# FFN-down of a decoder trunk: sums of the seven-product squares formed by GpSimd transfers in a two-slot ring, a fourth pair of half buffers, and 8, 8, 8, 5 squares for 7, 7, 7, 4

## The chip, the cores and the metric

The kernel runs on one core of one Trainium2 chip. The metric is the device time of one execution in microseconds; a measurement is the median of three runs. The core has a matrix engine (TensorE, "PE" in the profile, with its weight loads as "PEld"), three engines for elementwise work (VectorE "DVE", ScalarE "ACT", GpSimd "POOL"), a SyncE ("SP") that here issues nearly all DMA transfers, and 16 DMA engines that move data between HBM and the on-chip SBUF. TensorE accumulates into PSUM banks. Each engine works through its own instructions in program order and waits on semaphores for what others make; a stall of one instruction holds everything queued behind it on that engine.

## The reference

One decoder layer over 256 tokens of width 2048, in float32. The change lies in the channel mixer:

```python
h2 = rms_norm(x, mlp_norm[i])
x = x + jnp.square(jax.nn.relu(h2 @ w_ffn_up[i])) @ w_ffn_down[i]
```

with `w_ffn_up` 2048x8192 and `w_ffn_down` 8192x2048. Ahead of it come two mixers (causal pooling and an RWKV-7 recurrence) and the product with `w_out`; behind it

```python
gate = jax.nn.sigmoid(rms_norm(x, ple_norm[i]) @ w_ple_gate[i])
x = x + gate * (p[i] @ w_ple_proj[i])
return rms_norm(x, final_norm)
```

## The kernel before, in words

**Products.** All large products run as split float32: a weight block is divided into a high half (ScalarE copy, rounded to fp32r) and a low half (VectorE: raw minus high), and each product is three 128x512 matmuls (high·high, high·low, low·high). A weight block thus costs one load, ScalarE time for its high half, VectorE time for its low half, and TensorE time.

**Order.** The Python code records the instructions; a scheduler lays them out per engine by priority, so that the splits of later blocks (raised priority, `tc.high_priority(20000)`) move ahead of other work. What one engine then does is a fixed list. Loads of weights go through `load_raw` on SP into a small rotating set of buffers.

**FFN.** `ffn_half(hf)` runs twice, for 4096 hidden columns each. It first makes eight `y` tiles (`gemm_wide`, up-projection, squared ReLU, split), and then two `down_sweep(hf, pair)`; `pair` is one half of the output columns (0 to 1023, or 1024 to 2047). In tile names, `d01` is half 0, pair 1, and a number behind it is the step, `kp`. A sweep has 16 steps. Step `kp` takes a 256x1024 piece of `w_ffn_down` as four quarter blocks of 128x512 (here w11, w12 from the upper 128 rows, w21, w22 from the lower) against two row blocks of activations for each of two token tiles (a11, a12; a21, a22). Done plainly these are eight products, 24 matmuls.

**Squares.** In some steps, those in `SEVEN`, the piece is multiplied in the Strassen-Winograd way: seven products of sums of blocks, 21 matmuls. The four sums of activations are made once for a half by `activation_sums` and used in both sweeps. The sums of weights (t1, t2, t3, t4 in the code) are made at each square by four VectorE instructions on 128x512 (lines 1269 to 1272) in the tile `td`; a square has seven quarter blocks to split where a plain step has four. Before the change 7, 7, 7 and 4 steps of the four sweeps are squares, 25 of 64. In the last sweep, `d11`, only steps 1, 3, 7 and 11 are.

**Buffers.** Split halves of a step sit in rotating pairs of tiles (`wh`, `wl` in pool `wp`, three pairs), one tile pair called "a", "b", "c", "d" after the place in a step. The last pair of a square, "d", is held instead in two tiles with the tag `graw`. Those two tiles also take loads that `keep` makes during `d11`, at its 6th, 9th, 12th and 15th step: the last quarter of `w_ple_gate`, loaded early (line 1170), split into `gk` tiles (lines 1174, 1175) that take over `y` tiles no longer needed.

**End of a sweep.** After its last square the four banks that hold only products of squares are folded into the residual `x` (the `add` calls); in `d11` the first half of the transposes for the gate follow there.

## Time and profile before

| | |
|---|---|
| median of 3 runs | 1180.36 us (1180.09 to 1181.29) |
| time of the profiled execution | 1180.25 us |
| its span, first to last instruction | 1178.2 us |
| mean granted TensorE clock | 0.998 |
| TensorE busy | 1162.5 us, 99% |
| VectorE busy | 873.3 us, 74% |
| ScalarE busy | 709.3 us, 60% |
| GpSimd busy | 13.7 us, 1% |

Engine times are sums over one profiled execution. A "busy" TensorE is one with some matmul in flight, so the share says that it never lacked work for long, and the number and the pitch of the matmuls set the time. By the timeline, the four down sweeps run from 557.9 us to about 728 us (`d00`, `d01`) and from about 903 us to about 1076 us (`d10`, `d11`), with the second up-projection between them and the gate behind. The first of the two up-projections starts after the product with `w_out`, which stands at about 330 us.

### The profile page before, as it was taken

To read this page: it belongs to the slowest core of one execution; us is meant where nothing else is said; L and a number is where in the kernel's file an instruction comes from. 1 tells how busy PE (TensorE), PEld (TensorE's weight loads), DVE (VectorE), ACT (ScalarE), POOL (GpSimd) and SP (SyncE) were. 2 spreads that over 40 slices of the span, in tenths; PEclk is the share of its full clock that TensorE was granted. 3 is DMA by queue.
4 is the path that set the end of the run, shared out by engine and by line. 5 is a ranking of instruction groups with operands and counts; after the bars stand their busy time and mean duration, and the time that the engine had idled before them with its cause. 6 is when DMAs were issued, how large, how long until landed. Compare 5 with 4: busy or idle time off the path is not lost.

```text
span 1178.2 us, 17287 instructions
## 1 busy us (share of the span) xinstructions
PE 1162.5 (99%) x6419; PEld 973.4 (83%) x6419; DVE 873.3 (74%) x1188; ACT 709.3 (60%) x1309; POOL 13.7 (1%) x73
## 2 busy tenths in 40 slices
...
GB/s 290 154 202 146 135 140 119 119 179 157 160 203 178 177 182 196 184 192 200 187 204 212 198 202 209 186 191 191 185 195 190 202 205 195 290 233 249 197 56 72
DMA packets 60756, 216.81 MB, mean 184 GB/s; under 512 B 6784, under 2 KB 7552, under 8 KB 60288
## 3 DMA queue, kind: packets, MB, share of 16 engines
...
q14 instruction: 34, 0.28, 0.1%
...
## 4 chain that ended last, share of the span: by engine, by line
PE 96%; ACT 1%; DVE 1%; DMA 0%; issue 0%; SPq 0%; POOL 0%; DVEq 0%; POOLq 0%
PE u_w L1112 20%; PE u_w L1117 10%; PE d_b L1231 7%; PE d_b L1229 7%; PE d_b L1230 7%; PE d_w L1231 2%; PE d_w L1229 2%; PE d_w L1230 2%; PE gt_b L242 2%; PE gt_b L241 2%; PE gt_b L238 2%; PE zk_b L241 1%; PE zk_b L242 1%; PE o_b L241 1%; PE o_b L242 1%; PE zv_b L238 1%
## 5 line engine op out<-in xcount | busy, mean ns | idle before, releaser
L1112 PE MATMUL u_w<-h,wh_u 128*128 128x512 f32 x1024 | 321.9, 395 | 0.0
L167 ACT ACTIVATE wh_u<-raw_u 128x512 fp32r<-128x512 f32 x256 | 147.5, 623 | 160.9 <-issue 98.2
L168 DVE TENSOR_TENSOR wl_u<-raw_u,wh_u 128x1024 fp32r<-128x1024 f32 x128 | 156.6, 1224 | 105.2 <-ACT wh_u L167 103.5
L1117 PEld LDWEIGHTS u_w<-h,wl_u 128*128 128x128 f32 x1024 | 192.4, 188 | 45.4
L1117 PE MATMUL u_w<-h,wl_u 128*128 128x256 f32 x1024 | 201.4, 278 | 0.0
L1112 PEld LDWEIGHTS u_w<-h,wh_u 128*128 128x128 f32 x1024 | 156.0, 189 | 0.1
L168 DVE TENSOR_TENSOR wl_gt<-raw_gt,wh_gt 128x1024 fp32r<-128x1024 f32 x24 | 29.4, 1224 | 23.2 <-ACT wh_gt L167 23.2
L167 ACT ACTIVATE wh_gt<-raw_gt 128x512 fp32r<-128x512 f32 x48 | 28.0, 638 | 23.1 <-PE gt_b L242 14.4
L241 PE MATMUL gt_b<-wh_gt,h 128*128 128x512 f32 x96 | 37.3, 389 | 0.0
L242 PE MATMUL gt_b<-wh_gt,h 128*128 128x512 f32 x96 | 37.3, 389 | 0.0
L168 DVE TENSOR_TENSOR wl_o<-raw_o,wh_o 128x1024 fp32r<-128x1024 f32 x16 | 19.6, 1222 | 12.9 <-ACT wh_o L167 9.9
L167 ACT ACTIVATE wh_o<-raw_o 128x512 fp32r<-128x512 f32 x32 | 18.4, 623 | 16.3 <-issue 8.5
L167 ACT ACTIVATE wh_zp<-raw_zp 128x512 fp32r<-128x512 f32 x32 | 18.6, 623 | 15.7 <-PE zp_b L242 7.2
L168 DVE TENSOR_TENSOR wl_zk<-raw_zk,wh_zk 128x1024 fp32r<-128x1024 f32 x16 | 19.4, 1220 | 10.4 <-ACT wh_zk L167 10.4
L241 PE MATMUL zk_b<-wh_zk,hTh 128*128 128x512 f32 x64 | 25.2, 394 | 1.4 <-ACT wh_zk L167 1.4
L241 PE MATMUL zv_b<-wh_zv,hTh 128*128 128x512 f32 x64 | 26.0, 406 | 0.0
L167 ACT ACTIVATE wh_zk<-raw_zk 128x512 fp32r<-128x512 f32 x32 | 18.4, 622 | 12.4 <-PE zv_b L242 4.0
L241 PE MATMUL zp_b<-wh_zp,hTh 128*128 128x512 f32 x64 | 25.7, 401 | 0.0
L238 PE MATMUL gt_b<-wl_gt,h 128*128 128x512 f32 x96 | 25.7, 389 | 0.0
L168 DVE TENSOR_TENSOR wl_zv<-raw_zv,wh_zv 128x1024 fp32r<-128x1024 f32 x16 | 19.4, 1218 | 8.2 <-ACT wh_zv L167 7.4
L241 PE MATMUL zr_b<-wh_zr,hTh 128*128 128x512 f32 x64 | 25.4, 397 | 0.0
L242 PE MATMUL zp_b<-wh_zp,hTl 128*128 128x512 f32 x64 | 25.0, 391 | 0.0
...
## 6 DMA issues: line engine op xcount, KB each, us to landing
raw_u<-in_w_ffn_up_dram SPq DMA_DIRECT2D x128, 512.0 KB, 3.5
raw_d<-in_w_ffn_down_dram SPq DMA_DIRECT2D x128, 512.0 KB, 4.3
raw_gt<-in_w_ple_gate_dram SPq DMA_DIRECT2D x24, 512.0 KB, 3.5
raw_zk<-in_w_in_dram SPq DMA_DIRECT2D x16, 512.0 KB, 3.7
raw_zr<-in_w_in_dram SPq DMA_DIRECT2D x16, 512.0 KB, 3.3
raw_zv<-in_w_in_dram SPq DMA_DIRECT2D x16, 512.0 KB, 3.3
raw_zp<-in_w_in_dram SPq DMA_DIRECT2D x16, 512.0 KB, 3.2
raw_o<-in_w_out_dram SPq DMA_DIRECT2D x16, 512.0 KB, 4.2
```

The source lines that it names most:

```text
L167: nc.scalar.activation(wh[:, a * 512 : (a + 1) * 512], raw[:, a * 512 : (a + 1) * 512], AF.Copy)
L168: nc.vector.tensor_tensor(wl, raw, wh.bitcast(F32), op=ALU.subtract)
L238: nc.tensor.matmul(banks[tt], ah[:, ts_], halves[a][1], start=False, stop=last)
L241: nc.tensor.matmul(banks[tt], ah[:, ts_], halves[a][0], start=i + a == 0, stop=False)
L242: nc.tensor.matmul(banks[tt], al[:, ts_], halves[a][0], start=False, stop=False)
L1112: nc.tensor.matmul(bank[:, ct, :].rearrange("p (s t) -> p s t", s=2), wh[:, cs[ct]], hl, start=k == 0, stop=False, skip_group_check=True,)
L1117: nc.tensor.matmul(bank[:, ct, 0:T], wl[:, cs[ct]], hl[:, 0, :], start=False, stop=k == 15, skip_group_check=True)
L1229: nc.tensor.matmul(banks[n], ah, wh, start=first, stop=False)
L1230: nc.tensor.matmul(banks[n], ah, wl, start=False, stop=False)
L1231: nc.tensor.matmul(banks[n], al, wh, start=False, stop=last)
```

## The change

Numbers of lines are those of the new file where the new code is meant.

- **Which steps are squares.** `SEVEN` becomes (1, 3, 4, 6, 8, 9, 11, 13) for three sweeps and (1, 3, 6, 9, 11) for `d11`: 29 squares. Steps 3 and 4, and 8 and 9, are now neighbours in three sweeps. The order in which `d01` visits its steps is changed to (0, 2, 1, 5, 3, 4, 7, 6, 10, 8, 9, 12, 11, 14, 13, 15).
- **Sums of weights.** The seven products are rewritten so that one sum, p1 = w11 + w12, is the plain sum of two stored quarter blocks, and the others follow from it by two VectorE instructions: t2 = p1 − w22 on 128x512 (line 1309), in place in p1's memory, and t43, which subtracts t2 from both quarter blocks of rx (w21 and w11) at once, on 128x1024 with t2 read twice (line 1311), in place in rx. Signs move into the activation sum s3 and into a new constant `ns2` = −s2 for the two final adds.
- **How p1 is made.** GpSimd issues two transfers from HBM: one plain into a slot of `ring` (line 1228), and one that adds into the same slot (line 1229, `accum_op=ALU.add`), after waiting for the first. `ring` has two slots of 128x512; `begin_sum` starts two sums ahead of the FFN, and one more behind each square, for the square two further on. A square's second panel, `ry`, is loaded by SP with 256 KB for 512 KB.
- **Buffers.** Every fourth half pair lies in a pair of tiles of its own (`wh4`, `wl4`): four pairs for three. The memory of the tile `td` becomes the fourth tile for activation sums. The tile for w2 takes the place of the one for w11 and shares its memory with the activation sums' work tile (`junk`). The small tiles `ph`, `pl` become one, `phl`, in the ring's memory behind the FFN.
- **Order of products.** In a square 1, 2, 3, 5, 6, 4, 7 for 1, 2, 3, 5, 7, 6, 4. In a plain step the products with w21 come first, and the lower row panel is loaded first. `w_ffn_down` is laid out anew in HBM for that.

```diff
@@ -1157,6 +1157,7 @@
         nc.vector.reciprocal(s2, s2)
+        nc.vector.tensor_scalar_mul(ns2, s2, -1.0)
     h3_box = []
@@ -1185,28 +1186,56 @@
-    SEVEN = (1, 3, 5, 7, 9, 11, 13)
-    s_slots = (0, 2, 5)
+    SEVEN = (1, 3, 4, 6, 8, 9, 11, 13)
+    s_slots = (0, 2, 5, 1)
+    ns2 = const.tile([128, 2], F32, name="ns2")
     def activation_sums(box, kp, r):
         i = SEVEN.index(kp)
         if i % 2 == 0:
-            st = a8(s_slots[i // 2], f"S{kp}", F32R) if i < 6 else fp.tile([128, 1024], F32R, tag="S", name=f"S{kp}")
-            box[kp] = box[SEVEN[min(i + 1, len(SEVEN) - 1)]] = st
+            box[kp] = box[SEVEN[min(i + 1, len(SEVEN) - 1)]] = a8(s_slots[i // 2], f"S{kp}", F32R)
         st = box[kp][:, i % 2 * 1024 : i % 2 * 1024 + 1024]
...
-        nc.vector.tensor_tensor(s3, a11, a21, op=ALU.subtract)
+        nc.vector.tensor_tensor(s3, a21, a11, op=ALU.subtract)
         nc.vector.tensor_tensor(s2_, s1, a11, op=ALU.subtract)
-    def down_sweep(hf, pair, ys, sboxes, hooks=(), between=None, seven=SEVEN):
+    ring = fp.tile([128, 1024], F32, tag="S", name="ring")
+    squares_of = {}
+    visits_of = {}
+    for hf in range(2):
+        for pair in range(2):
+            last = hf + pair == 2
+            squares_of[hf, pair] = (1, 3, 6, 9, 11) if last else SEVEN
+            visits_of[hf, pair] = (0, 2, 1, 4, 3, *range(5, 16)) if last else (range(16), (0, 2, 1, 5, 3, 4, 7, 6, 10, 8, 9, 12, 11, 14, 13, 15))[pair]
+    in_line = [(*hp, kp) for hp, visits in visits_of.items() for kp in visits if kp in squares_of[hp]]
+    begun = []
+    turns = []
+    def slot(n):
+        return ring[:, n % 2 * 512 : n % 2 * 512 + 512]
+    def begin_sum():
+        n = len(begun)
+        if n < len(in_line):
+            hf, pair, kp = in_line[n]
+            nc.gpsimd.dma_start(slot(n), w_down[pair, hf * 16 + kp, 1, :, 1, :])
+            nc.gpsimd.dma_start(slot(n), w_down[pair, hf * 16 + kp, 0, :, 1, :], accum_op=ALU.add)
+            begun.append(n)
+    def summed(*square):
+        return slot(in_line.index(square))
+    def down_sweep(hf, pair, ys, sboxes, hooks=(), between=None):
         nm = f"d{hf}{pair}"
+        seven, visits = squares_of[hf, pair], visits_of[hf, pair]
         hooks = dict(hooks)
         b2, b4, b3, bx = (mm_bank(f"{nm}_b{i}") for i in range(4))
         w16, w57 = (wide_bank(f"{nm}_w{i}") for i in range(2))
@@ -1230,11 +1259,16 @@
             nc.tensor.matmul(banks[n], ah, wl, start=False, stop=False)
             nc.tensor.matmul(banks[n], al, wh, start=False, stop=last)
+        def half_tiles(name):
+            turns.append(name)
+            if len(turns) % 4 == 0:
+                return [fp.tile([128, 1024], F32R, tag=f"{hl}4", name=f"{hl}_{name}") for hl in ("wh", "wl")]
+            return [wp.tile([128, 1024], F32R, tag=hl, name=f"{hl}_{name}") for hl in ("wh", "wl")]
         def halves_of(src, name, own=False):
-            pool, kw = (fp, dict(bufs=2)) if own else (wp, {})
-            wh = pool.tile([128, 1024], F32R, tag="graw" if own else "wh", name=f"wh_{name}", **kw)
-            wl = pool.tile([128, 1024], F32R, tag="graw" if own else "wl", name=f"wl_{name}", **kw)
+            wh, wl = [fp.tile([128, 1024], F32R, tag="graw", bufs=2, name=f"{hl}_{name}") for hl in ("wh", "wl")] if own else half_tiles(name)
             with tc.high_priority(20000):
                 for c in range(2):
                     nc.scalar.activation(wh[:, c * 512 : c * 512 + 512], src[:, c * 512 : c * 512 + 512], AF.Copy)
@@ -1245,43 +1279,49 @@
             o = pair * 1024 + c * 512
             return xr[tt][:, o : o + 512]
-        def add(tt, c, src):
-            nc.vector.scalar_tensor_tensor(xs(tt, c), src, s2[:, tt : tt + 1], xs(tt, c), op0=ALU.mult, op1=ALU.add)
-        for q, kp in enumerate(((0, 2, 1, 4, 3, *range(5, 16)) if hf else (0, 2, 1, 4, 3, 6, 5, 8, 7, 10, 9, 12, 11, 14, 13, 15)) if pair else range(16)):
+        def add(tt, c, src, scale=s2):
+            nc.vector.scalar_tensor_tensor(xs(tt, c), src, scale[:, tt : tt + 1], xs(tt, c), op0=ALU.mult, op1=ALU.add)
+        def panel(kp, c, name, rows):
+            return load_raw(w_down[pair, hf * 16 + kp, c, :, 0:rows].rearrange("p r n -> p (r n)"), rows * 512, name)
+        for q, kp in enumerate(visits):
             if q in hooks:
                 hooks[q]()
             y, j = ys[kp // 2], kp % 2 * 512
             a11, a21, a12, a22 = ((y[:, j + i * 128 : j + i * 128 + 128], y[:, 1024 + j + i * 128 : 1152 + j + i * 128]) for i in range(4))
-            rx, ry = (load_raw(w_down[pair, hf * 32 + 2 * kp + i], 1024, f"{nm}_{kp}_{i}") for i in range(2))
+            rx, ry = (panel(kp, c, f"{nm}_{kp}_{c}", 1 if c and kp in seven else 2) for c in range(2))
             if kp in seven:
                 i = SEVEN.index(kp)
                 st = sboxes[kp][:, i % 2 * 1024 : i % 2 * 1024 + 1024]
                 s1, s2_, s3, s4 = ((st[:, c * 128 : c * 128 + 128], st[:, 512 + c * 128 : 640 + c * 128]) for c in range(4))
-                t_ = a8(1, f"t{nm}_{kp}")
-                t1, t3, t2, t4 = (t_[:, c * 512 : c * 512 + 512] for c in range(4))
-                wa = fp.tile([128, 1024], F32R, tag="wa", name=f"wa{nm}_{kp}")
-                w11 = wa[:, 0:512], wa[:, 512:1024]
+                p1 = summed(hf, pair, kp)
+                t2 = p1
+                wa = fp.tile([128, 1024], F32R, tag="junk", bufs=1, name=f"wa{nm}_{kp}")
+                w2 = wa[:, 0:512], wa[:, 512:1024]
+                w21, w11 = halves_of(rx, f"{nm}_{kp}a")
+                wh, wl = half_tiles(f"{nm}_{kp}b")
+                w22, w1 = ((wh[:, c : c + 512], wl[:, c : c + 512]) for c in (0, 512))
                 with tc.high_priority(20000):
-                    split_sb(*w11, rx[:, 0:512])
-                w21, w22 = halves_of(ry, f"{nm}_{kp}b")
-                with tc.high_priority(20000):
-                    nc.vector.tensor_tensor(t1, rx[:, 512:1024], rx[:, 0:512], op=ALU.subtract)
-                    nc.vector.tensor_tensor(t3, ry[:, 512:1024], rx[:, 512:1024], op=ALU.subtract)
-                    nc.vector.tensor_tensor(t2, t3, rx[:, 0:512], op=ALU.add)
-                    nc.vector.tensor_tensor(t4, ry[:, 0:512], t2, op=ALU.subtract)
-                w1, w3 = halves_of(t_[:, 0:1024], f"{nm}_{kp}c")
-                w2, w4 = halves_of(t_[:, 1024:2048], f"{nm}_{kp}d", True)
-                for n, a_, w_ in (("1", a11, w11), ("2", a12, w21), ("3", s4, w22), ("5", s1, w1), ("7", s3, w3), ("6", s2_, w2), ("4", a22, w4)):
+                    split_sb(*w22, ry[:, 0:512])
+                    split_sb(*w1, p1)
+                    nc.vector.tensor_tensor(t2, p1, ry[:, 0:512], op=ALU.subtract)
+                    t43 = rx.rearrange("p (r n) -> p r n", r=2)
+                    nc.vector.tensor_tensor(t43, t43, t2.unsqueeze(1).to_broadcast([128, 2, 512]), op=ALU.subtract)
+                    split_sb(*w2, t2)
+                w4, w3 = halves_of(rx, f"{nm}_{kp}d", True)
+                for n, a_, w_ in (("1", a11, w11), ("2", a12, w21), ("3", s4, w22), ("5", s1, w1), ("6", s2_, w2), ("4", a22, w4), ("7", s3, w3)):
                     prod(n, a_, w_)
+                begin_sum()
             else:
-                w11, w12 = halves_of(rx, f"{nm}_{kp}a")
-                for n, a_, w_ in (("2", a11, w11), ("4", a21, w11), ("3", a11, w12), ("x", a21, w12)):
+                w21, w11 = halves_of(rx, f"{nm}_{kp}a")
+                for n, a_, w_ in (("2", a12, w21), ("4", a22, w21), ("2", a11, w11), ("4", a21, w11)):
                     prod(n, a_, w_)
-                w21, w22 = halves_of(ry, f"{nm}_{kp}b")
-                for n, a_, w_ in (("2", a12, w21), ("4", a22, w21), ("3", a12, w22), ("x", a22, w22)):
+                w22, w12 = halves_of(ry, f"{nm}_{kp}b")
+                for n, a_, w_ in (("3", a12, w22), ("x", a22, w22), ("3", a11, w12), ("x", a21, w12)):
                     prod(n, a_, w_)
-            if kp == seven[-1]:
+            if kp == max(seven):
                 u = fp.tile([128, 512], F32, tag="r", bufs=2, name=f"u{nm}")
                 with tc.high_priority(20000):
                     add(0, 0, b1)
@@ -1289,10 +1329,10 @@
                     nc.vector.tensor_tensor(u, b6, u, op=ALU.add)
                     add(0, 1, b5)
                     add(1, 1, b5)
-                    add(0, 1, u)
+                    add(0, 1, u, ns2)
                     nc.vector.tensor_tensor(u, b7, u, op=ALU.add)
                 add(1, 0, u)
-                add(1, 1, u)
+                add(1, 1, u, ns2)
                 if between is not None:
                     between()
         for n, tt, c in (("2", 0, 0), ("4", 1, 0), ("3", 0, 1), ("x", 1, 1)):
@@ -1329,17 +1369,20 @@
         if hf == 0:
             down_sweep(hf, 1, ys, sboxes)
         else:
-            down_sweep(hf, 1, ys, sboxes, {5: keep, 8: keep, 11: keep, 14: keep}, lambda: [h3_part("ple_norm", n) for n in range(2)], (1, 3, 7, 11))
+            down_sweep(hf, 1, ys, sboxes, {5: keep, 8: keep, 11: keep, 14: keep}, lambda: [h3_part("ple_norm", n) for n in range(2)])
+    for _ in range(2):
+        begin_sum()
     ffn_half(0)
     ffn_half(1)
     h3 = h3_box[0]
     praw = load_raw(pT.rearrange("p a t -> p (a t)"), 512, "pT")
-    ph, pl = (fp.tile([128, 512], F32R, tag=nm, name=nm) for nm in ("ph", "pl"))
+    phl = fp.tile([128, 1024], F32R, tag="S", name="phl")
+    ph, pl = phl[:, 0:512], phl[:, 512:1024]
     split_sb(ph, pl, praw[:, 0:512])
     pp = [a8(1 + tt, f"pp{tt}") for tt in range(2)]
     for n in range(4):
@@ -1462,7 +1505,7 @@
...
-        "w_ffn_down": a["w_ffn_down"][0].reshape(64, 128, 2, 1024).transpose(2, 0, 1, 3),
+        "w_ffn_down": a["w_ffn_down"][0].reshape(32, 2, 128, 2, 2, 512)[:, ::-1].transpose(3, 0, 4, 2, 1, 5),
```

What the change does to the order of instructions is seen at three places. First ScalarE ahead of the FFN, in the product with `w_out` (`o3a`, `o0` are its panels; `ring` is the new tile). Of the new kernel:

```order
L167 ACTIVATE wh_o3a_0_3311<-raw_o3a_0_3309 128x512 x2
L167 ACTIVATE wh_o3a_1_3330<-raw_o3a_1_3328 128x512 x2
L172 ACTIVATE wh_d00_1b_5475<-ring_3750 128x512
L167 ACTIVATE wh_o0_6_3364<-raw_o0_6_3362 128x512 x2
L167 ACTIVATE wh_o0_7_3383<-raw_o0_7_3381 128x512 x2
```

In the kernel before, the split of `o0_6` stands right behind `o3a_1`; now the split of the first sum, of a square more than 200 us later, stands between them.

Second GpSimd's list, which held no transfers (from its last earlier work on; the pairs go on alternating to the end):

```order
L804 COPY tE_t_2736<-AR1_1500 128x6x64 x2
L1228 DMA ring_3750<-in_w_ffn_down_dram 128x512 x2
L1229 DMA ring_3750<-in_w_ffn_down_dram 128x512 x2
L1228 DMA ring_3750<-in_w_ffn_down_dram 128x512
L1229 DMA ring_3750<-in_w_ffn_down_dram 128x512
```

GpSimd now has 58 transfers, two for each square.

Third VectorE in `d11`, where the first load of `keep` is split (`gk0`, from `graw0`). Before:

```order
L1241 TENSOR_TENSOR wl_d11_6b_9429<-raw_d11_6_1_9409,wh_d11_6b_9428 128x1024
L1241 TENSOR_TENSOR wl_d11_7b_9454<-raw_d11_7_1_9447,wh_d11_7b_9453 128x1024
L1175 TENSOR_TENSOR gk0_9365<-graw0_9363,gk0_9365 128x1024
L1241 TENSOR_TENSOR wl_d11_7d_9468<-td11_7_9449,wh_d11_7d_9467 128x1024
L1241 TENSOR_TENSOR wl_d11_7c_9463<-td11_7_9449,wh_d11_7c_9462 128x1024
L1241 TENSOR_TENSOR wl_d11_8a_9504<-raw_d11_8_0_9499,wh_d11_8a_9503 128x1024
```

and with the change:

```order
L173 TENSOR_TENSOR wad11_6_9462<-ring_3750,wad11_6_9462 128x512
L1275 TENSOR_TENSOR wl_d11_7a_9511<-raw_d11_7_0_9506,wh_d11_7a_9510 128x1024
L1176 TENSOR_TENSOR gk0_9416<-graw0_9414,gk0_9416 128x1024
L1275 TENSOR_TENSOR wl_d11_7b_9528<-raw_d11_7_1_9508,wh_d11_7b_9527 128x1024
L1275 TENSOR_TENSOR wl_d11_6d_9479<-raw_d11_6_0_9458,wh_d11_6d_9478 128x1024
L1275 TENSOR_TENSOR wl_d11_8a_9555<-raw_d11_8_0_9550,wh_d11_8a_9554 128x1024
```

Before, the last half pair of a square behind this load was that of step 7; now it is that of step 6, one step nearer to the load, and the split of `gk0` and of step 7's second pair stand ahead of it. The same rows stand around `gk2` and square 11 (`wl_d11_12a`, `gk2`, `wl_d11_12b`, `wl_d11_11d`).

## The prediction

> **What bounds the kernel now.** I read the page's busy lines and the chain of waits first, then a table of stretches for the down sweeps, then single rows of the timeline. The profiled execution took 1180.25 us for a span of 1178.2 us; the 2.05 us around the span I take as unchanged. Its time lies 0.11 us under the median of the runs, 1180.36, so changes are worked out in the trace and the sum is put on the median.
>
> ```profile
> span 1178.2 us, 17287 instructions
> PE 1162.5 (99%) x6419; PEld 973.4 (83%) x6419; DVE 873.3 (74%) x1188; ACT 709.3 (60%) x1309; POOL 13.7 (1%) x73
> PE 96%; ACT 1%; DVE 1%; DMA 0%; issue 0%; SPq 0%; POOL 0%; DVEq 0%; POOLq 0%
> ```
>
> The chain that ends last is 96% TensorE. So a matmul taken away shortens the span by its pitch, as long as its weights still come in time. The stretches that hold three of the sweeps and then `d11` with the start of the gate say how much room the others have:
>
> ```profile
> core 0: us, PE busy (x) PEld busy (x) DVE busy (x) ACT busy (x) POOL busy (x), PEclk, DMA share, GB/s
> 557.80:643.00 85.20, 85.20 (x379) 70.59 (x378) 74.25 (x86) 50.81 (x88) 0.00 (x0) 1.00 0.56 197
> 643.00:728.00 85.00, 85.00 (x384) 70.57 (x383) 74.73 (x85) 50.27 (x87) 0.00 (x0) 1.00 0.58 205
> 903.00:988.00 85.00, 85.00 (x377) 70.38 (x376) 75.22 (x88) 50.40 (x88) 0.00 (x0) 1.00 0.55 196
> 988.00:1076.00 88.00, 88.00 (x402) 72.42 (x401) 74.61 (x86) 58.99 (x111) 0.00 (x0) 1.00 0.72 258
> ```
>
> TensorE is busy without a break at clock 1.00, VectorE for 88% (75 of 85), the DMA engines for 55 to 72%. VectorE is the engine that would bound next.
>
> **The main term.** A square has 21 matmuls and a plain step 24; four more squares (29 for 25) are 12 matmuls fewer. What one is worth is the distance of starts, not its shown duration:
>
> ```profile
> 557.93 0.40 PE L1229 MATMUL d_b<-wh_d_0a,y 128*128 128x512 f32 x1
> ...
> 563.38 0.39 PE L1229 MATMUL d_w<-wad,y 128*128 128x512 f32 x1
> ```
>
> These rows open step 0 and step 1 of `d00`, 24 matmuls apart: 5.45 / 24 = 0.227 us each (the 0.39 us is a latency; three run at once). 12 × 0.227 = **2.72 us** to gain.
>
> **VectorE.** The four sums are dropped; of what comes, only the two-for-one subtraction has a form of its own.
>
> ```profile
> L1269 DVE TENSOR_TENSOR td<-raw_d 128x512 f32<-128x512 f32 x25 | 17.3, 691 | 2.3 <-DMA raw_d<-in_w_ffn_down_dram 1.7
> L1241 DVE TENSOR_TENSOR wl_d_1d<-td,wh_d_1d 128x1024 fp32r<-128x1024 f32 x4 | 4.9, 1221 | 1.4 <-ACT wh_d_1d L1240 1.4
> 563.79 0.68 DVE L1269 TENSOR_TENSOR td<-raw_d 128x512 f32<-128x512 f32 x1
> 564.39 0.69 DVE L1270 TENSOR_TENSOR td<-raw_d,raw_d 128x512 f32<-128x512 f32 x1
> 564.99 1.22 DVE L1241 TENSOR_TENSOR wl_d_2a<-raw_d,wh_d_2a 128x1024 fp32r<-128x1024 f32 x1
> 566.13 0.68 DVE L173 TENSOR_TENSOR wad<-raw_d,wad 128x512 fp32r<-128x512 f32 x1
> L676 DVE TENSOR_TENSOR SC<-sc,cmask 128x512 f32<-128x512 f32 x16 | 10.3, 681 | 4.6 <-PE sc L669 4.5
> ```
>
> Back to back, 512 columns pass every 0.60 us and 1024 every 1.14. A square before: five of 512 and three of 1024, 5 × 0.60 + 3 × 1.14 = 6.42 us. Now t2, t43, three splits of 512 (w22, w1, w2) and two of 1024 (a, d): 4 × 0.60 + 3 × 1.14 = 5.82 us, if t43 costs like a plain 1024. A plain step stays at 2.28. A sweep's weights (the rest of the 74 to 75 us are the adds and what else falls in the stretch) go from 7 × 6.42 + 9 × 2.28 = 65.5 to 8 × 5.82 + 8 × 2.28 = 64.8 us, while TensorE's sweep falls from 363 × 0.227 = 82.4 to 360 × 0.227 = 81.7. VectorE doesn't become the bound. t43, which reads t2 twice, isn't in the trace; in L676 every operand is new and 512 columns cost the same 681 ns, so I take 1.14, with 2.28 as the upper end. ScalarE splits the same seven quarter blocks per square: 8 × 7 + 8 × 4 = 88 for 85 in a sweep, 3 × 0.6 = 2 us more on an engine with 34 us free in 85. Those are covered by TensorE and cost nothing by themselves.
>
> **Where squares are neighbours** (3, 4 and 8, 9, in three sweeps: six places) the cover is thinner. The "d" half pair lies in the two `graw` tiles, which the earlier square gives back only with its last matmul. Counted from there: the tiles of 5a come free when the square's first two products are over, 15 × 0.227 = 3.4 us earlier; ScalarE needs 0.2 + 1.15 us, so VectorE has 5a at −2.0 us, and then 5a, t43, w2 of square 4, 5b and 4d take 4 × 1.14 + 0.60 + 0.1 = 5.3 us: done at 3.3 us. Product 4's low half is the 17th matmul of the next square, wanted at 16 × 0.227 = 3.63 us. The margin is 0.3 us, so nothing is lost; with t43 at 2.28 each place would lose 0.8 us, 4.8 in all.
>
> **GpSimd's transfers.** 58 transfers of 256 KB, in pairs of which the second waits for the first. Neither a transfer from GpSimd nor an adding one stands in the trace. The nearest are 256 KB from SP:
>
> ```profile
> wa<-in_wa_up_dram SPq DMA_DIRECT2D x2, 256.0 KB, 2.7
> xq<-in_xT_dram SPq DMA_DIRECT2D x1, 256.0 KB, 5.7
> raw_d<-in_w_ffn_down_dram SPq DMA_DIRECT2D x128, 512.0 KB, 4.3
> ```
>
> So a sum takes 5.4 to 11.4 us; I take 8 to 9, twice the 4.3 us of the loads in this very stage. The slot is free when VectorE has split w2, about at the square's fifth product; its next user stands two squares on. The tightest distance, square 1 to square 4, is two steps and some, about 12 us ahead of the split; elsewhere some 17. SP's load of `ry` is halved, so a square moves 1280 KB for 1024: 8 × 0.25 MB in 82 us add 26 GB/s to 200, less than the 258 that `d11` carries without a break in TensorE. Cost 0; above 12 us per sum, each microsecond is one of TensorE at six places.
>
> The Trainium skill ("SBUF — State Buffer", section "Who interferes with whom") speaks against such transfers: their descriptors are written by GpSimd, which is shut out while VectorE runs in a two-port mode, though it counts two-input instructions, which is what the sweeps run, as harmless here. No row before shows either. By its harmless side the sum stays as it is; by the other, rival two below would come.
>
> **The first sum.** Its split stands in ScalarE's list between `o3a` and `o0_6` (see the order above), and all splits of the `w_out` product queue behind it. The ring's memory is that of weights read until `pm`:
>
> ```profile
> 316.91 0.28 PE L182 MATMUL pm<-d,pws 128*128 128x256 f32 x1
> 321.82 1.15 ACT L167 ACTIVATE wh_o3a<-raw_o3a 128x512 fp32r<-128x512 f32 x2 [1.62 <-issue]
> 324.54 1.15 ACT L167 ACTIVATE wh_o<-raw_o 128x512 fp32r<-128x512 f32 x2 [1.57 <-issue]
> 330.64 0.39 PE L241 MATMUL o_b<-wh_o,mg 128*128 128x512 f32 x1
> ```
>
> The transfers start at about 317.2. TensorE wants `wh_o` at 330.64, that is a sum by 330.64 − 1.15 − 0.6 = 328.9: 11.7 us. With 5.4 to 11.4 us it comes at 322.6 to 328.6, and ScalarE and VectorE take it in their idle time. Cost 0, with up to 2 us at the upper end, once.
>
> **The gate's loads in `d11`.** This is where I expect a loss. `keep` loads into the `graw` tile that square 3 has given back, and 6d needs that tile after `gk0` has been split from it.
>
> ```profile
> 1009.03 0.35 SPq L1170 DMA_DIRECT2D graw<-in_w_ple_gate_dram  x1
> 1016.20 1.15 ACT L1174 ACTIVATE gk<-graw 128x512 fp32r<-128x512 f32 x2 [0.29 <-DMA graw<-in_w_ple_gate_dram]
> 1017.38 1.23 DVE L1175 TENSOR_TENSOR gk<-graw,gk 128x1024 fp32r<-128x1024 f32 x1 [0.22 <-ACT gk L1174]
> DMA to landing us min/median/max: 4.0/5.1/7.1
> ```
>
> Before, the next user was square 7. Now, from the end of step 5: ScalarE splits 7b (its tiles are given back then) for 0.2 + 1.15 us, VectorE 7b and 6d for 1.14 + 1.22 and 0.03 to 0.1 between: 3.79 us against 3.63 wanted, 0.16 lost at the least. The load can start only with square 3's end, 24 × 0.227 = 5.44 us before the end of step 5; behind its landing stand `gk0` and 7b on ScalarE (2.3 us), then 7b and 6d on VectorE (2.36). So the loss is the landing time less 4.4 us: 0.16 at 4.0, 0.7 at 5.1, 2.7 at 7.1 (that one stood behind the 1 MB load `fn`, which now stands behind it). Square 11 meets `gk2` in the same way. Two places: 0.3 to 5.4 us; I take 0.3 each, **0.6 us**, nearer the lower end because the load `fn` no longer stands ahead.
>
> **Sum.** 2.72 − 0.6 = 2.1 us less: 1180.25 − 2.1 = 1178.1 in the profiled execution, 1178.2 as median. That is −0.18%. A measurement of this kernel tells about 0.2%, 2.4 us, from no change, so the forecast is "same", just short of "faster".
>
> **Rivals.** *One: every wait is hidden.* The loads land in 4 us and the whole 2.72 us comes, less 0.2: 1177.6 to 1177.8, faster. For it speaks that TensorE has no break in any of the sweeps; against it the 0.16 us that the order of `d11` alone forces.
>
> *Two: the sums come late, slower.* GpSimd's transfer or the adding one is slower than SP's, each sum takes more than 12 us, and ScalarE, waiting for the ring in fixed order, holds every later split. At 13.5 us a pair, six places lose 1.5 us each, 9 us, and the first sum 1.8: 1180.4 − 2.1 + 10.8 = 1189. It passes 1182.7 (slower) from 12.6 us. For it: two transfers in series behind 55% busy engines, and 5.7 us has been seen for one. Against: the median of twice as many bytes is 4.3. The lock-out of the Trainium skill's page above would show in this way.
>
> *Three: the splits fall behind.* t43 at double cost, 4.8 us at the neighbours, or late gate loads, 2.7 us twice: 1180.4 − 2.1 + 4.8 = 1183.1, or about 1182.5; half of it lands at 1180, no change. Against: L676 at the plain price.
>
> *Four: a matmul is worth its 0.39 us.* 12 × 0.39 = 4.7, 1176.3 after the losses. The starts speak against it.
>
> **Chances.** The forecast 0.40; rival one 0.27; two 0.15; three 0.14; four 0.04. Faster by over 0.2%: rival one (most of it), four, and the forecast's lower edge, 0.36. Slower: two, and the full size of three, 0.20. The rest, 0.44, within 0.2%. The range goes from 1176.8, which holds rival one and a little more, to 1182.5, where three ends and two begins. The forecast's own range is 1177.4 to 1179.6.
>
> **What would show it.** In the new trace: 12 matmul rows fewer and the sweeps at 0.227 us a matmul; VectorE's L1311 at 1.2 us; GpSimd's pairs landing under 9 us, no idle time of ScalarE or TensorE put down to `ring`; TensorE idle only in `d11`, for some tenths before product 4 of squares 6 and 11, put down to `wl_d_6d` and `wl_d_11d`. I would be wrong if TensorE waits in `d00`, `d01` or `d10`, or if ScalarE stands at `wh_d_1b<-ring` beyond 329 us.

## The result, and the profile after

The change makes the kernel slower: 1189.49 us as the median of four runs (1186.49 to 1190.51) against 1180.39 (1180.09 to 1181.29) for the kernel before, a ratio of 1.0072 [1.0051, 1.0092]. The forecast was 1178.2 with a range up to 1182.5. The profiled execution is the shortest of the four, 1186.49 us, with a span of 1184.4 for 1178.2 before. The trace therefore accounts for 6.2 us of the 9.1; the other three runs are another 2 to 4 us longer and have no trace.

The matmuls that open and close the sweeps tell in which stage the time came. From the timeline of TensorE, first of the kernel before, then of the changed one:

```profile
722.32 0.39 PE L1231 MATMUL d_b<-wh_d_15b,y 128*128 128x512 f32 x1
900.88 0.40 PE L1229 MATMUL d_b<-wh_d_0a,y 128*128 128x512 f32 x1
1069.41 0.40 PE L1231 MATMUL d_b<-wh_d_15b,y 128*128 128x512 f32 x1
```

```profile
559.13 0.40 PE L1258 MATMUL d_b<-wh_d_0a,y 128*128 128x512 f32 x1
722.16 0.39 PE L1260 MATMUL d_b<-wh_d_15b,y 128*128 128x512 f32 x1
900.72 0.40 PE L1258 MATMUL d_b<-wh_d_0a,y 128*128 128x512 f32 x1
1074.25 0.40 PE L1260 MATMUL d_b<-wh_d_15b,y 128*128 128x512 f32 x1
```

| stretch, by starts of matmuls | before | after | difference |
|---|---|---|---|
| up to the first matmul of `d00` | 557.93 | 559.13 | +1.20 |
| `d00` and `d01` | 164.39 | 163.03 | −1.36 |
| second up-projection | 178.56 | 178.56 | 0 |
| `d10` and `d11` | 168.53 | 173.53 | +5.00 |
| behind, to the end of the span | 108.76 | 110.20 | +1.44 |

`d00` and `d01` give exactly what was promised: six matmuls fewer at 0.227 us are 1.36. `d10` and `d11` have six fewer too, so a stall of 6.36 us stands there, and in `d00`, `d01` and `d10` no distance of starts passes 0.26 us: all of it is in `d11`. The stretches say the same. Of the changed kernel, in the order of columns of the prediction's table:

```profile
557.80:643.00 85.20, 85.20 (x379) 70.59 (x379) 77.34 (x86) 52.38 (x92) 11.53 (x16) 1.00 0.76 232
643.00:728.00 85.00, 85.00 (x384) 70.62 (x384) 76.17 (x86) 51.28 (x91) 11.47 (x16) 1.00 0.73 227
903.00:988.00 85.00, 85.00 (x376) 70.37 (x375) 76.91 (x86) 51.79 (x92) 11.49 (x16) 1.00 0.76 232
988.00:1080.00 92.00, 87.33 (x386) 70.50 (x385) 74.88 (x86) 58.64 (x110) 4.30 (x6) 0.98 0.73 246
```

TensorE stays busy without a break in three sweeps, with VectorE at 91% (77.3 of 85.2) and the DMA engines at 73 to 76% for 55 to 58. In the fourth it lacks 4.7 us and the granted clock falls to 0.98. The chain of waits, 96% TensorE before, names what else now ends last:

```profile
PE 89%; DVE 3%; DMA 3%; ACT 2%; issue 1%; SPq 0%; DVEq 0%; ACTq 0%
```

From the product with `w_out` on, the new waits of TensorE are five (us in total, times, longest):

```profile
PE d_b L1259 <- DVE wl_d_11d L1275: 1.8, 1, 1.8
PE d_b L1259 <- DVE wl_d_9d L1275: 1.3, 1, 1.3
PE o_b L241 <- ACT wh_o L167: 0.8, 1, 0.8
PE d_b L1259 <- DVE wl_d_6d L1275: 0.6, 1, 0.6
PE h3t L1134 <- DVE x L1283: 0.5, 1, 0.5
```

So there are two places: the product with `w_out`, where the first sum stands in ScalarE's list, and the "d" halves of the three squares 6, 9 and 11 of `d11`. The transposes `h3t` behind the sweep come late with them: in `r_five` (below), where TensorE waits for no half pair, the stretch behind the sweeps takes 108.90 us, for 108.76 before the change.

**The first sum.** From the timelines of GpSimd and ScalarE in the changed kernel:

```profile
317.94 1.27 POOL L1228 DMA_DIRECT2D ring<-in_w_ffn_down_dram  x2 [62.63 <-PE pm L182]
323.46 0.89 POOL L1229 DMA_DIRECT2D ring<-in_w_ffn_down_dram  x1 [4.26 <-DMA ring<-in_w_ffn_down_dram]
330.53 0.63 ACT L172 ACTIVATE wh_d_1b<-ring 128x512 fp32r<-128x512 f32 x1 [7.45 <-DMA ring<-in_w_ffn_down_dram]
331.06 3.22 ACT L167 ACTIVATE wh_o<-raw_o 128x512 fp32r<-128x512 f32 x6
```

Both slots' plain transfers go out at 317.94, the first adding one at 323.46, and the sum is there at 330.53: 12.6 us. ScalarE stands idle for 7.45 us in front of it, and the splits of `wh_o`, for which TensorE waits, queue behind. This is the very row that the prediction named as its refutation ("beyond 329 us"). In the sweeps a pair is quicker:

```profile
581.04 0.57 POOL L1228 DMA_DIRECT2D ring<-in_w_ffn_down_dram  x1 [2.79 <-DVE wad L173]
585.75 0.89 POOL L1229 DMA_DIRECT2D ring<-in_w_ffn_down_dram  x1 [4.14 <-DMA ring<-in_w_ffn_down_dram]
...
ring<-in_w_ffn_down_dram POOLq DMA_DIRECT2D x58, 256.0 KB, 4.6
```

with the plain one landed 4.7 us after its issue and 4.6 as the median of all 58, some 9 us a pair.

**The last sweep.** SP's, ScalarE's and VectorE's rows around step 9 of `d11`:

```profile
1009.84 0.38 SPq L1396 DMA_DIRECT2D fn<-in_final_norm_dram  x1
1014.22 4.10 SPq L158 DMA_DIRECT2D raw_d<-in_w_ffn_down_dram  x3
1019.24 0.33 SPq L1171 DMA_DIRECT2D graw<-in_w_ple_gate_dram  x1
```

```profile
1023.45 1.15 ACT L1274 ACTIVATE wh_d_9a<-raw_d 128x512 fp32r<-128x512 f32 x2 [5.72 <-DMA raw_d<-in_w_ffn_down_dram]
1027.11 1.15 ACT L1175 ACTIVATE gk<-graw 128x512 fp32r<-128x512 f32 x2 [2.50 <-DMA graw<-in_w_ple_gate_dram]
```

```profile
1016.74 1.22 DVE L1275 TENSOR_TENSOR wl_d_6d<-raw_d,wh_d_6d 128x1024 fp32r<-128x1024 f32 x1
1024.63 1.23 DVE L1275 TENSOR_TENSOR wl_d_9a<-raw_d,wh_d_9a 128x1024 fp32r<-128x1024 f32 x1 [4.40 <-ACT wh_d_9a L1274]
1028.29 1.23 DVE L1176 TENSOR_TENSOR gk<-graw,gk 128x1024 fp32r<-128x1024 f32 x1 [2.43 <-ACT gk L1175]
1034.36 1.22 DVE L1275 TENSOR_TENSOR wl_d_9d<-raw_d,wh_d_9d 128x1024 fp32r<-128x1024 f32 x1
1046.91 1.22 DVE L1275 TENSOR_TENSOR wl_d_11d<-raw_d,wh_d_11d 128x1024 fp32r<-128x1024 f32 x1
```

Square 6 keeps t43 in the memory of its own load `rx`, so that buffer is given back only when VectorE has made `wl_d_6d`, at 1017.96. The third transfer of the 1014.22 row, the first panel of step 9, is issued right then (1017.99) and lands at 1023.45, 5.5 us later. Beside it the gate's second block takes from 1019.24 to 1027.1, 7.9 us. VectorE, in fixed order, stands still for 4.40 and 2.43 us; ScalarE comes late as well, and 9d is made at 1034.36 and 11d at 1046.91, each too late. Of the two waits the second is the last one ahead of 9d: behind the gate's second block VectorE works without a pause up to 9d. The first is only in part the panel's. 9a also takes the tiles of 7a, whose last matmul starts at 1021.77, so by an estimate 9a could not have been split before about 1022.2 (in `u_free`, below, where 9a waits for TensorE, it starts 0.43 us behind that matmul). At 6d it is the gate's first block: issued at 1008.14, split from 1013.27 on, 5.13 us.

The last stall has a tail. Rows of TensorE and one stretch:

```profile
1045.96 0.39 PE L1258 MATMUL d_w<-wh_d_11d,S 128*128 128x512 f32 x1
1048.19 0.50 PE L1259 MATMUL d_b<-wl_d_11d,y 128*128 128x512 f32 x1 [1.84 <-DVE wl_d_11d L1275]
...
1050.32 0.63 PE L1258 MATMUL d_b<-wh_d_12a,y 128*128 128x512 f32 x1
1050.74 0.63 PE L1259 MATMUL d_b<-wl_d_12a,y 128*128 128x512 f32 x1
...
1050.00:1052.00 2.00, 2.00 (x6) 1.46 (x5) 2.00 (x4) 0.00 (x0) 0.00 (x0) 0.50 0.87 322
```

From about 1.3 us after the stall TensorE runs at a clock of 0.50, at 0.42 us a matmul, for some 3.4 us: 1.7 us lost. Worked out from the distances of starts, less 0.227: 6d 0.77, the product with `wad` in square 9 0.25, 9d 1.48, 11d 2.00, the half clock 1.70. That is 6.2 of the 6.36 us.

### The profile page after: what moved, and what is told of

Same layout as the page of the kernel before. It is cut to its first block, busy times and chain, and to the rows that moved or that the text cites. A ratio compares the mean times of both kernels' runs of the same rounds, so it can differ in the third digit from the quotient of the medians.

```text
span 1184.4 us, 17395 instructions
## 1 busy us (share of the span) xinstructions
PE 1163.5 (98%) x6407; PEld 971.7 (82%) x6407; DVE 877.7 (74%) x1194; ACT 714.7 (60%) x1323; POOL 55.7 (5%) x131
## 4 chain that ended last, share of the span: by engine, by line
PE 89%; DVE 3%; DMA 3%; ACT 2%; issue 1%; SPq 0%; DVEq 0%; ACTq 0%
PE u_w L1112 20%; PE u_w L1117 10%; PE d_b L1259 7%; PE d_b L1260 6%; PE d_b L1258 6%; PE d_w L1259 2%; PE d_w L1260 2%; PE d_w L1258 2%; PE gt_b L242 2%; PE gt_b L241 2%; PE gt_b L238 2%; PE o_b L241 1%; PE o_b L242 1%; PE zv_b L238 1%; PE o_b L238 1%; PE zp_b L238 1%
## 5 line engine op out<-in xcount | busy, mean ns | idle before, releaser
L167 ACT ACTIVATE wh_u<-raw_u 128x512 fp32r<-128x512 f32 x256 | 147.5, 623 | 158.5 <-issue 98.6
L168 DVE TENSOR_TENSOR wl_u<-raw_u,wh_u 128x1024 fp32r<-128x1024 f32 x128 | 156.7, 1224 | 106.7 <-ACT wh_u L167 105.0
L1228 POOL DMA_DIRECT2D ring<-in_w_ffn_down_dram x29 | 16.6, 574 | 616.0 <-DVE raw_d L1311 237.8
L172 ACT ACTIVATE wad<-ring 128x512 fp32r<-128x512 f32 x29 | 18.2, 628 | 44.1 <-DVE ring L1309 41.2
L1311 DVE TENSOR_TENSOR raw_d<-raw_d,ring 128x1024 f32<-128x1024 f32 x29 | 35.5, 1224 | 0.7
L1229 POOL DMA_DIRECT2D ring<-in_w_ffn_down_dram x29 | 25.2, 869 | 106.4 <-DMA ring<-in_w_ffn_down_dram 106.4
L167 ACT ACTIVATE wh_zp<-raw_zp 128x512 fp32r<-128x512 f32 x32 | 18.6, 623 | 16.0 <-PE zp_b L242 7.1
```

The costliest lines, as they stand in the source:

```text
L167: nc.scalar.activation(wh[:, a * 512 : (a + 1) * 512], raw[:, a * 512 : (a + 1) * 512], AF.Copy)
L168: nc.vector.tensor_tensor(wl, raw, wh.bitcast(F32), op=ALU.subtract)
L1229: nc.gpsimd.dma_start(slot(n), w_down[pair, hf * 16 + kp, 0, :, 1, :], accum_op=ALU.add)
L1311: nc.vector.tensor_tensor(t43, t43, t2.unsqueeze(1).to_broadcast([128, 2, 512]), op=ALU.subtract)
```

## The experiments

All edits are made to the changed kernel; each time is a median beside that of the kernel before in the same session.

### Where the first sum's wait comes from

The theory was that the two transfers are too slow for the split's place in ScalarE's list. The first edit starts them later, in the first up-projection, behind the making of `s2` (one element of each slot is written from `s2`, which sets the time):

```diff
+                for n in range(2):
+                    nc.vector.tensor_copy(slot(n)[:, 0:1], s2[:, n : n + 1])
+                    begin_sum()
...
-    for _ in range(2):
-        begin_sum()
```

> The changed kernel with its first two sums begun later: each slot of the ring gets one element written from s2, which exists only when the second up-panel is through, before its transfers start; so the split of the first sum leaves ScalarE's list ahead of the product with w_out and stands some 70 rows later. Theory A (the loss has two places: the first sum ahead of the up-projection, 1.0 to 1.2 us in the trace, and d11 with the gate's loads, about 7.5): TensorE's 1.2 us gap before o_b is gone, the time falls by about 1.2 us from the changed kernel's 1189.5, to some 1188, and d11 keeps its gaps. Theory B (GpSimd's transfers hold up the engines wherever they run): nothing falls, since the transfers only move.

Measured: 1187.79 us for 1180.64, 1.0060 [1.0045, 1.0074]. The gap in the product with `w_out` is gone and stands in the up-projection instead. GpSimd's, ScalarE's and the waits' rows:

```profile
446.18 1.27 POOL L1228 DMA_DIRECT2D ring<-in_w_ffn_down_dram  x2 [189.14 <-ACT wh_u L167]
456.93 0.63 ACT L172 ACTIVATE wh_d_1b<-ring 128x512 fp32r<-128x512 f32 x1 [7.00 <-DMA ring<-in_w_ffn_down_dram]
PE u_w L1112 <- ACT wh_u L167: 1.3, 1, 1.3
```

The split moved with the transfers, to 10.75 us behind them, and is again too early. So the place is no accident of the `w_out` product. It looks as if the scheduler puts a raised split where its own reckoning has the data landed, and the chip needs longer; that reckoning is inferred. It can do so only because the split's target is free. Square 1's "b" pair is the fourth half pair taken, the first in the new tiles `wh4` and `wl4`, which nothing has used before.

The second edit therefore gives the new tiles to the first half pair instead, which is split from a plain load; the fourth then waits for a tile of the old three:

```diff
-            if len(turns) % 4 == 0:
+            if len(turns) % 4 == 1:
```

> The changed kernel with one digit altered: of each four half pairs the first and not the fourth lies in the tiles of its own. In the changed kernel the fourth is 1b of d00, whose tiles are free from the start, so that nothing but the ring keeps its split from being listed ahead of the up-projection; now 1b has a pair that the up-projection still uses, and its split stands at the end of the up-projection. The transfers start as early as before. Theory A (the split in the wrong place of the lists, not the transfers, costs the first 1.0 to 2.1 us, and a later start only moved the wait into the up-projection): TensorE's gap before o_b is gone and none comes instead; 1 to 2 us less than the changed kernel, 1187.5 to 1188.5 with d11's loss left. Theory B (the transfers disturb by running): no change, 1189.5.

Measured: 1185.76 us for 1180.58, 1.0040 [1.0025, 1.0054]. The transfers start at 319.33, as before, and the split now stands where its square is:

```profile
559.91 0.61 ACT L172 ACTIVATE wh_d_1b<-ring 128x512 fp32r<-128x512 f32 x1
```

No wait stands at `o_b`, and the loss of `d11` is as before (`d10` and `d11` 173.46 us). The first matmul of `d00` still starts at 559.40, because this trace has a stretch at half clock from 38.6 to 42.0 us, long before the FFN, which the trace of the changed kernel lacks. The price of the split's place was measured by itself in a version without the stalls of `d11` (`r_five`, below) by taking only this edit back:

```diff
-            if len(turns) % 4 == 1:
+            if len(turns) % 4 == 0:
```

> Five early squares in d11 with four half pairs, the gate's loads behind them and fn late, but the split of the first sum left where the change put it (the fourth of four pairs in tiles of its own). Against the same kernel with the split in its place (1179.6 us) this prices that place alone. Theory A: 1.0 to 2.1 us, the gap before o_b in the traces, 1180.6 to 1181.7. Theory C (it costs more than its gap, since the stall changes what follows): 3 us or more, 1182.5 and above.

Measured: 1181.72 us for 1181.02, 1.0002 [0.9993, 1.0011], where `r_five` has 1179.56 for 1181.01. The difference of the two differences is 0.70 + 1.45 = 2.15 us (by the two intervals some 1.5 us more or less), and the trace shows a distance of starts of 2.08 at `o_b`, with

```profile
333.29 0.63 ACT L172 ACTIVATE wh_d_1b<-ring 128x512 fp32r<-128x512 f32 x1 [8.32 <-DMA ring<-in_w_ffn_down_dram]
```

The first sum's place thus costs 1.0 us in the profiled execution of the changed kernel and some 2.1 here; it goes with how long the two pairs take.

### What stalls the last sweep

Rivals: the squares' places in `d11` (five for four); the load `fn`, 1 MB, in front of step 9's panel; the gate's blocks in the `graw` tiles. The first edit takes the squares to four and away from each other, by which 6d is not behind `gk0`:

```diff
-            squares_of[hf, pair] = (1, 3, 6, 9, 11) if last else SEVEN
+            squares_of[hf, pair] = (1, 3, 8, 11) if last else SEVEN
```

> The changed kernel with four squares in d11, steps 1, 3, 8 and 11, for five (1, 3, 6, 9, 11): 28 squares, 3 matmuls more. VectorE then splits gk0 and gk1 ahead of square 8's last half pair with plain steps between, as the kernel before had it with 7. Theory A: the gaps in d11 (0.8, 1.5, 2.0 us and 1.4 us of half clock) and at the transposes behind it (1.2 us) go, 0.7 us of matmuls comes back: 1189.5 - 6.9 + 0.7 = about 1183. Theory B: only the 0.7 us is added, and one sum of 29 is gone: 1189 to 1190.

Measured: 1184.02 us, 1.0025 [1.0016, 1.0034], 3.8 us better than `a_first` in the same session. `d10` and `d11` take 170.06 us, 3.5 less than in the changed kernel though three matmuls more. Half pairs are hardly waited for any more (0.39 us between starts at 11d); 0.8 and 0.9 us appear at `h3t`. With `a_first` added:

> Both edits: first sums begun after the second up-panel, and squares 1, 3, 8, 11 in d11. 28 squares for 25 are 9 matmuls fewer than before, 9 x 0.227 = 2.0 us. Theory A: nothing else is left of the loss, 1180.4 - 2.0 = 1178.4 us, and no gap of TensorE in any sweep. Theory B: well above 1180.4, 1187 or so.

1186.99 us, 1.0048 [1.0036, 1.0061]. The edits don't add up: the moved wait is now longer than the one it replaces, and it has a tail. The wait and the stretch behind it:

```profile
PE u_w L1112 <- ACT wh_u L167: 1.8, 1, 1.8
460.00:462.00 2.00, 1.85 (x6) 1.66 (x7) 2.00 (x4) 1.43 (x3) 0.00 (x0) 0.50 0.45 109
```

Here too the clock is at one half, for 6.8 us, behind distances of starts of 2.07 and 1.40 us.

Next, five squares as in the change, with `fn` held back until the last gate block is split (its load goes into the same memory, behind this copy):

```diff
+    hold = a8(0, "hold")
+    nc.vector.tensor_copy(hold[:, 0:1], kept[3][0][0][:, 0:1].bitcast(F32))
```

> The changed kernel, but the 1 MB load of the final norm's weights (fn), which in the changed kernel starts in d11 between the loads of the gate and of step 9, waits until the fourth kept gate block is split. Theory A1 (d11 loses because its loads come late behind that megabyte): square 9's gap of 1.5 us goes and 11's shrinks, 3 to 5 us less than the changed kernel: 1185 to 1186. Theory A2 (d11 loses because step 9's first panel gets its buffer only when 6d has been split, t43 being made in place in that buffer): the gaps at 9 and 11 stay, less than 1 us is gained: 1188.5 or more.

Measured: 1184.32 us, 1.0032 [1.0022, 1.0042]; `d10` and `d11` 171.35. The distance at 9d falls from 1.70 to 0.95 us and there is no half clock, but ScalarE's wait ahead of it stays, and so does 11d:

```profile
1024.30 1.15 ACT L1274 ACTIVATE wh_d_9a<-raw_d 128x512 fp32r<-128x512 f32 x2 [5.99 <-DMA raw_d<-in_w_ffn_down_dram]
PE d_b L1259 <- DVE wl_d_11d L1275: 1.9, 1, 1.9
```

So `fn` is a good part of the loss without being its root. In the trace `d10` and `d11` are 2.2 us shorter and the stretch behind them 0.7; by the ratios the gain is some 4 us, with wide intervals. That the half clock is missing need not be its doing: the second trace of the changed kernel (below) lacks it too. Then the gate's first four blocks in memory of their own, so that none takes a `graw` tile (`fn` shares that memory and comes behind them):

```diff
+    kraw = []
...
+        if kp < 4:
+            if kp == 0:
+                kraw.append(a8(0, "kraw"))
+            raw = kraw[0][:, kp % 2 * 1024 : kp % 2 * 1024 + 1024]
+        else:
+            raw = fp.tile([128, 1024], F32, tag="graw", bufs=2, name=f"graw{kp}")
```

> The changed kernel with the four gate blocks of d11 loaded into halves of a tile of their own (the memory of activation sums no longer needed, which fn took; fn is loaded after the fourth is split): the last half pair of a square no longer waits for a gate block. 29 squares stay. Theory A (the shared graw tiles are what d11 loses by): the gaps before wl_d_6d, 9d and 11d go, with the half clock behind 11 and most of the wait of the transposes, 6 to 7 us less, 1183. Theory A2 (VectorE, or a panel's buffer held until 6d is split, is too slow for squares at 6, 9 and 11 even so): some gaps stay, 1185 to 1187.

Measured: 1185.56 us, 1.0040 [1.0027, 1.0053]; `d10` and `d11` 172.61. The waits at 6d and 11d are gone, so these two do come from the shared tiles. At 9d the distance is 1.70 again, but from another wait: the blocks now load earlier and are split earlier in ScalarE's list, which stands for two of them, 2.33 and here 3.71 us. That the distance is the same is no chance: in VectorE's list the split of 10a stands between those of `wad` and 9d, so 9d's distance is 1.70 us as soon as `wad` is late too, and what is late beyond that shows at `wad` (1.11 us between starts here, 0.48 in the changed kernel). With three distances of 0.65, 1.13 and 1.76 us at `h3t` this takes back most of what 6d and 11d gave:

```profile
1028.17 1.15 ACT L1181 ACTIVATE gk<-kraw 128x512 fp32r<-128x512 f32 x2 [3.71 <-DMA kraw<-in_w_ple_gate_dram]
```

With `f_turn` added:

> 29 squares, with the first of four pairs in tiles of its own and the gate blocks in a tile of their own. Theory A: all of the loss is gone and 12 matmuls are left as gain, 1180.4 - 2.7 = 1177.7; 1 to 2 us more if the transposes still wait. Theory A2: 1183 to 1185.

1182.57 us, 1.0018 [1.0010, 1.0026], with the same wait of 1.3 us at 9d and a distance of 2.29 us at one `h3t`.

Neither of these frees the buffer that step 9 waits for. The next does: t43 of square 6 is written elsewhere (into the tile of sums that `d11` no longer needs). Two other things move with it: `fn`, which follows in that tile, comes later, and the split of the gate's second block now stands behind those of 9b.

```diff
+                    rows = rx.rearrange("p (r n) -> p r n", r=2)
+                    if (hf, pair, kp) == (1, 1, 6):
+                        rx = a8(0, "t6")[:, 0:1024]
                     t43 = rx.rearrange("p (r n) -> p r n", r=2)
-                    nc.vector.tensor_tensor(t43, t43, t2.unsqueeze(1).to_broadcast([128, 2, 512]), op=ALU.subtract)
+                    nc.vector.tensor_tensor(t43, rows, t2.unsqueeze(1).to_broadcast([128, 2, 512]), op=ALU.subtract)
```

> One change to the changed kernel: in square 6 of d11 the two-for-one subtraction t43 is written into other memory (a tile whose activation sums are no longer needed there) and not over the load rx. The load buffer is then free when t43 is made, about 7 us earlier than the split 6d that frees it now; the load fn, which lies in the same tile, comes behind square 6. To be read against the run with fn late alone (1184.3 us; d10 and d11 171.35 us; distances of starts 0.84 at 6d, 0.95 at 9d, 2.27 at 11d; ScalarE idle 5.99 us for raw_d at 9a). Theory, the held buffer delays step 9's first panel: ScalarE's wait for raw_d at 9a falls below 2 us, the distance at 9d to under 0.4, and with the lag gone 11d falls as well, to under 1.5; d10 and d11 take 169.5 to 170.7 us, the median is 1182.3 to 1183.6. Rival, the panel is late for another reason (the gate's blocks beside it, or SP's own order): 9a still waits 4 us or more, 9d stays at 0.8 to 1.0, d10 and d11 at 171 to 171.7, median 1184 to 1184.7.

Measured: 1184.51 us for 1181.06, 1.0032 [1.0021, 1.0043]; `d10` and `d11` 173.02. Since the edit holds `fn` back too, this stands against `e_fnlate` with the same ratio: the load comes earlier, and the time does not fall. Step 9's first panel is issued at 1010.11 for 1017.99, ScalarE no longer waits for it, and there is no gap at 9d; 11d falls to 1.26. But 6d rises to 2.22, with the half clock behind it:

```profile
1007.53 0.33 SPq L1171 DMA_DIRECT2D graw<-in_w_ple_gate_dram  x1
1013.88 1.15 ACT L1175 ACTIVATE gk<-graw 128x512 fp32r<-128x512 f32 x2 [1.51 <-DMA graw<-in_w_ple_gate_dram]
1024.43 1.15 ACT L1274 ACTIVATE wh_d_9a<-raw_d 128x512 fp32r<-128x512 f32 x2 [6.27 <-PE d_b L1260]
1033.76 1.22 DVE L1275 TENSOR_TENSOR wl_d_9d<-raw_d,wh_d_9d 128x1024 fp32r<-128x1024 f32 x1
PE d_b L1259 <- DVE wl_d_6d L1275: 1.8, 1, 1.8
```

The gate's first block took 6.35 us here; step 9's panel, issued 2.6 us behind it, now runs beside it, and whether that lengthens it one trace doesn't show. The split of 9a then waits for TensorE, itself late by that stall. Counted from the first matmul of `d10` (900.09 here, 900.72 in the changed kernel), VectorE begins 9d after 133.7 us here and after 133.6 there, and TensorE gets 11d's low half after 147.8 and 147.5. So the gap at 9d is gone because TensorE comes to step 9 later, by 2.9 us, and not because 9d is made earlier: what freeing the buffer is worth is not shown.

The traces show what ties 9d and 11d together. From the end of its last wait in step 9, which is for the gate's second block, VectorE takes 18.6 us until it begins 11d in the changed kernel, 18.7 in `e_fnlate` and 18.5 in the second trace of the changed kernel (below). Both places are late by the same lag. In `e_fnlate` that block landed after 6.8 us, for 7.9, and 11d is begun 1.2 us earlier, counted from the first matmul of `d10`.

The term at 6d is settled by the times in which the first block landed, since the prediction's rule, landing less 4.4 us, can be read against six traces:

| | landing (issue to split) | less 4.4 | distance at 6d less 0.227 |
|---|---|---|---|
| `e_fnlate` | 4.98 | 0.58 | 0.61 |
| the changed kernel | 5.13 | 0.73 | 0.77 |
| `f_turn` | 5.17 | 0.77 | 0.80 |
| `a_first` | 5.54 | 1.14 | 1.17 |
| the changed kernel again (below) | 5.78 | 1.38 | 1.42 |
| `u_free` | 6.35 | 1.95 | 1.99 |

Below these landings the rule doesn't go on: in `e_fnlate` ScalarE waited only 0.19 us for the block, so an earlier landing could not have saved more than that of the 0.61.

Last, the changed kernel with nothing edited, for a second trace:

> The changed kernel itself, unedited, with a second profile. Open are the 2 to 4 us that three of its four runs took over the profiled one (1186.49 us). If they are the same waits at other lengths, a profile at 1188 us or more shows the first sum's distance at o_b at 1.5 to 2.3 us (for 1.1) and the d11 waits longer or with more of the half clock, and the up-projections and the other three sweeps unchanged (178.56 us, 163.0 us for d00 and d01). If they come from somewhere else, the stretches outside d11 and o_b are longer, for instance d00 and d01 at 164 us or more, or the up-projection over 179.

Measured: 1187.63 us for 1181.06, 1.0064 [1.0042, 1.0085], the profiled execution 1187.14. The two first sweeps take 163.00 us and the second up-projection 178.56, as in the first trace. The waits are the same with other lengths: distances of starts of 1.91 us at `o_b` (1.22 in the first trace), 1.64 at 6d (1.00), 1.67 at 9d (1.70), 2.10 at 11d (2.23), 2.21 at the `h3t` behind 14a (0.23), and no half clock.

```profile
PE h3t L1134 <- DVE h L1141: 2.2, 2, 1.8
PE o_b L241 <- ACT wh_o L167: 1.5, 1, 1.5
```

### How much of the gain can be had

The three mended together: `f_turn`, four squares of `b_four`, `fn` late.

> Three edits together: the first of four pairs in tiles of its own, squares 1, 3, 8, 11 in d11, and fn loaded after the fourth gate block. 28 squares, 9 matmuls fewer than before. Theory A: 1180.4 - 2.0 = 1178.4 if the transposes' wait behind d11 goes too, 1180 to 1181 if it stays as with the four squares alone (2 us in d11, 1 us behind it). Theory B: 1184 as with the four squares alone.

1181.96 us for 1180.58, 1.0010 [1.0002, 1.0019]. What remains are a distance of 1.09 us at 11d and what `h3t` waits for on VectorE:

```profile
PE h3t L1134 <- DVE h L1141: 1.4, 1, 1.4
```

Four pairs of half buffers let the splits run further ahead in VectorE's list, in front of what `h3t` needs. If that is it, three pairs in `d11` bring it back:

```diff
-            if len(turns) % 4 == 0:
+            if len(turns) % 4 == 1 and not name.startswith("d11"):
```

> The three edits (split of the first sum in its place, squares 1, 3, 8, 11 in d11, fn loaded late) with three half pairs in d11 in place of four. In d11 that kernel still lost 5.3 us against its matmuls' pitch, mostly in three waits: 0.9 us before wl_d_11d, 0.9 and 1.6 us at the gate's transposes, which wait for VectorE to fold the banks of the squares into x. Theory A (the fourth pair lets the splits of steps 12 and 13 run ahead of those adds): in VectorE's list the adds now stand ahead of 13a and partly of 12b, the transposes' waits shrink by 1 to 2.5 us, 1179.5 to 1181. Theory B (VectorE is simply behind by then, through the gate blocks it waits for): no change against the 1182.0 of the three edits, or slower.

1180.08 us for 1181.01, 0.9990 [0.9982, 0.9999]: the first that isn't slower, and `h3t` waits 0.3 us; distances of 0.84 and 0.82 us remain before `wad` and 11d of square 11. The other way is to have the squares early in `d11`, and the gate's blocks behind the last of them, when the `graw` tiles are free for good. With four squares, (1, 3, 4, 6), and the blocks at the 9th, 11th, 13th and 15th step (with `f_turn` and `fn` late, its copy on GpSimd):

```diff
+            squares_of[hf, pair] = (1, 3, 4, 6) if last else SEVEN
+            visits_of[hf, pair] = (0, 2, 1, 5, 3, 4, 7, 6, *range(8, 16)) if last else ...
+            down_sweep(hf, 1, ys, sboxes, {8: keep, 10: keep, 12: keep, 14: keep}, ...
```

> Four squares in d11, but early: steps 1, 3, 4, 6 (visited as 1, 5, 3, 4, 7, 6), and the gate's loads only behind the last square, at the 9th, 11th, 13th and 15th step; the split of the first sum in its place, fn late. So no half pair of a square ever takes turns with a gate block. 28 squares, 9 matmuls fewer than before. Theory A (what is left of the loss comes of squares standing between the gate's loads): no wait of TensorE over 0.3 us in d11, 1180.5 - 2.0 = 1178.5. Theory B (the changed square is itself too heavy beside d11's other work): 1181 or more.

1180.94 us for 1181.01, 0.9998 [0.9990, 1.0007]. No half pair is waited for in `d11`; one distance of 1.78 us at `h3t` is left. And with all five, the full count of the change:

```diff
+            squares_of[hf, pair] = (1, 3, 4, 6, 8) if last else SEVEN
+            visits_of[hf, pair] = (0, 2, 1, 5, 3, 4, 7, 6, 9, 8, *range(10, 16)) if last else ...
+            down_sweep(hf, 1, ys, sboxes, {10: keep, 11: keep, 13: keep, 14: keep}, ...
```

> The same with five squares in d11: steps 1, 3, 4, 6, 8, visited as 1, 5, 3, 4, 7, 6, 9, 8, and the gate's loads at the 11th, 12th, 14th and 15th step. All 29 squares of the change, 12 matmuls fewer than before. Theory A: 1180.5 - 2.7 = 1177.8, or some tenths more where four gate blocks now crowd into the last five steps. Theory B: 1182 or more.

1179.56 us for 1181.01, 0.9985 [0.9975, 0.9994], a span of 1176.7, and one wait left in `d11`. So five squares as such are not too many there: with no gate block between them, no half pair is waited for:

```profile
span 1176.7 us, 17395 instructions
PE h3t L1134 <- DVE h L1141: 1.2, 1, 1.2
```

With three pairs in `d11` on top:

> Five early squares in d11 with the gate's loads behind them, the split of the first sum in its place, fn late, and three half pairs in d11 for four. With four pairs one wait of TensorE was left there, 1.3 us at the gate's first transposes, behind splits that ran ahead of the adds. Theory A: the adds now stand ahead of the splits of steps 11 and 12, the wait goes, and the whole of the 12 matmuls is left: 1181.0 - 2.7 = 1178.3, 1.3 us under the same kernel with four pairs (1179.6). Theory B: the fourth pair has nothing to do with it, or d11 needs it: 1179.6 or more.

1178.91 us for 1181.02, 0.9984 [0.9976, 0.9993]. `h3t` is down to a distance of 0.47 us, but waits of some tenths appear at neighbouring squares (0.60 at 4d of `d10`), so by the ratio the two are the same. Both beat the kernel before, with intervals that just exclude 1, by 1.5 to 2.1 us of the 2.72 that the matmuls promise.

## Why the prediction was wrong

**The main term held.** 0.227 us a matmul, 12 fewer: `d00` and `d01` show 1.36 us, and so would the other half without its stalls. (The prediction's "three run at once" doesn't come out of its rows: 0.39 us at a pitch of 0.227 is two at a time. The sum doesn't use it.)

**VectorE held.** t43 takes 1224 ns, the price of a plain 1024, as taken; the neighbours, with a margin of 0.3 us, lose nothing in this kernel.

```profile
L1311 DVE TENSOR_TENSOR raw_d<-raw_d,ring 128x1024 f32<-128x1024 f32 x29 | 35.5, 1224 | 0.7
```

**GpSimd's transfers held in the sweeps.** About 9 us a pair, no wait for `ring` in any of them. Rival two had the number, 1189, and not the mechanism: it lost 9 us at six places in the sweeps, where nothing is lost; only its 1.8 us for the first sum came. What the Trainium skill ("SBUF — State Buffer", section "Who interferes with whom") calls harmless, two-input instructions beside transfers from GpSimd, cost no wait in the sweeps, with VectorE 91% busy and 256 KB landing in 4.6 us.

**The first sum failed.** The step gave it 5.4 to 11.4 us against 11.7 due, "cost 0, with up to 2 us at the upper end". The bound came from single transfers of SP, one after the other; here two pairs ran together, in a stretch in which the DMA engines were busy for 96%, and the first took 12.6 us. Which of the two made it slow isn't shown. The upper end came within 0.3 us of the limit and was still counted as nothing in the sum. The wait measured 1.0 us in the changed kernel's first trace and up to 1.9 in others. The step also took the split's place as given; the runs show that it follows from a target tile that was free.

**The gate's loads failed most.** The term was 0.6 us, at 6d and 11d, with an upper end of 5.4; it is 6.36 us, and 1.44 more behind. At 6d the rule was right to 0.04 us and the landing wrong: 0.3 us meant 4.7 us, where the prediction's own row had a median of 5.1, which gives the 0.7 us that came. The landings as a whole did not change (median of the eight gate blocks 5.2 us, for 5.1 before); the one ahead of 6d took 5.0 to 6.35 in six traces. "Nearer the lower end because the load `fn` no longer stands ahead" dropped a load that now starts 1.7 us behind that block, and holding it back took the ratio from 1.0072 and 1.0064 to 1.0032. At 11d and at 9d the rule itself was wrong, in three ways. Square 9 wasn't on the list: it meets the gate's second block, whose load starts when square 6 gives its tile back (1019.24) and which is the last wait ahead of 9d. Its first panel comes late as well, because t43 made in place holds the load buffer of `rx`; the prediction followed the tiles that the diff names (`graw`, `wh4`, `ring`) and not the one whose use it lengthens. Then each place was reckoned as if VectorE and ScalarE came to it on time; after 6.8 us of idle time VectorE was late at both. And the stall's tail at half clock, 1.70 us, was in no term; it came in one of the changed kernel's two traces. Rival three, with late gate loads at 2.7 us twice, was the nearest mechanism, too small by the same omissions.

**What stays open.** The changed kernel's eight timed runs lie between 1186.05 and 1190.51 us. Its two traces put the differences into the same waits, which change by up to 2 us from one execution to the next, and into the half clock that comes or not; the longest runs themselves have no trace, so that this holds for them is argued and not shown. A rival is the half clock long before the FFN: 7 of the 17 traces, all of edited kernels, have it for 3.4 us somewhere between 37 and 43 us, and `f_turn`, which has it, starts `d00` 1.9 us later than `h_best`, which has the same first sum and lacks it. The adding transfer wasn't priced by itself. At 9d the gate's second block is the last wait; what the held buffer and `fn` add to it isn't parted.
